# Loading a rotation table through ScalarE's queue, three slots sooner

## The chip, the cores and the metric

The kernel runs on one core of one Trainium2 chip. The metric is the device time of one execution in microseconds; lower is better. The core has five engines with a queue of instructions each: TensorE (PE, with the weight loads as PEld), VectorE (DVE), ScalarE (ACT), GpSimd (POOL) and SyncE (SP). They run side by side and wait for each other by semaphores. SyncE, ScalarE and GpSimd issue DMA transfers; 16 DMA engines carry these out. In the profile q1 is the DMA queue of SyncE's transfers, q10 that of ScalarE's, and q0 that of GpSimd's.

## The reference

The reference is an encoder trunk of two layers over 512 tokens of width 1024. Each layer normalizes the tokens, projects them once into mixer heads, memory query heads and a gate, attends, gates the heads, projects back and adds the result. The first layer's mixer is dilated window attention, the second's is grouped-query attention. The first layer's part that the change bears on is this:

```python
qkv = qkv.reshape(Bn, S, 3, N_A_GROUPS, A_HEADS, HEAD_DIM)
q = rmsnorm(qkv[:, :, 0], qn_g[:, None, :])
k = rmsnorm(qkv[:, :, 1], kn_g[:, None, :])
q = apply_rope(q, ang) * (HEAD_DIM ** -0.5)
k = apply_rope(k, ang)
```

Only the first 32 of the 128 columns of a head are rotated (`apply_rope` with 16 angles), so a token needs 16 cosines and 16 sines, and the norm gains qn_g and kn_g of the three groups for those 32 columns.

## The kernel before

**Tiling.** Tokens stand in four blocks of 128. A matrix product in float32 is made of three products in a shorter float: each weight tile wl (128x1024) is split by ScalarE into a high part wh (L333) and by VectorE into a low part wo (L347), and TensorE multiplies wh with the high and the low part of the activations (L178, L179) and wo with the high part (L182). The big projections (`s_chunk`) use the seven products of Strassen's scheme for 2x2 blocks, so sums of weight tiles are needed. Such sums are made by VectorE (L291) or by accumulating DMA transfers that GpSimd issues (L260, L296, L306). Plain weight loads are issued by SyncE (L260). Four wh and four wo tiles are kept in a ring.

**Order.** The order on every engine is written out by the program. A `Driver` counts slots; a slot ends when TensorE has done one group of products, which is 12 products of 512 columns in this part of the program. Side work is a generator that is given to the driver with a delay in slots and yields the number of slots until its next step. Within a slot the steps run in the order in which they were given. So slots fix the order of instructions on an engine, and not a time.

**The table.** `setup()` is such a generator, given with the delay `SET_AT`. Its first step issues three DMA loads: the table of cosines and sines (tabA, 128 rows of 1 KB, read as `(a i) f -> i a f` with i = 4, L1255) and the first 32 columns of the gains, broadcast to 128 partitions (grA, twice 128 x 3 rows of 128 B, L1256 for the queries' qn and L1257 for the keys' kn). Its second step scales the query gains on VectorE (L1263, which reads what L1256 loaded), and its third multiplies table and gains into the table that is used later (L1266, twice, which reads all three).

**Around it.** The first step falls in the projection of the first group's values. SyncE's queue holds weight loads and, at L1341, the stores of the finished value tiles to v0r in HBM. ScalarE's holds the casts L333, casts of activations (L671), and the copies L415 out of PSUM. VectorE's holds the low parts L347, sums of activations (L683, L685), low parts of activations (L674), the sums L438 out of PSUM, and parts of the memory keys and values (L753, L756, L790).

**Counters.** The transfers of SyncE and ScalarE use eight semaphores in turn, in the order in which the program names them; the instruction rows call them DMAHW0 to DMAHW7. A transfer waits until the one before it on its semaphore has landed. GpSimd's use eight others (DMASW). The suffix _49 means nothing here.

## Time and profile before

| What | Value |
|---|---|
| median of 3 runs | 933.24 us (933.13 to 934.04) |
| the profiled execution, its own time | 933.17 us |
| its span, first to last instruction | 931.4 us |
| TensorE busy | 924.8 us, 99% |
| VectorE busy | 801.7 us, 86% |
| ScalarE busy | 695.7 us, 75% |
| GpSimd busy | 360.5 us, 39% |
| packets of q1, q0, q10 | 60744, 20384, 1968 |
| granted TensorE clock | 1.0 |

Busy times are unions of an engine's instructions, without its sequencer's own work such as issuing a DMA. A timeline row has the start, the duration, the engine and line, the operation, the tiles as output <- inputs, and the number of instructions merged in it; in square brackets stands the idle time of the engine before it and what ended it. A `q` behind an engine's name marks its sequencer. A row of a DMA queue has its packets, their megabytes, and the time they took as a share of 16 engines; a packet is one row of a transfer, or one of the 4-byte marks with which a transfer reports its end.

### The profile page before, as it was taken

What the parts mean: (1) busy time and instruction counts of PE and PEld (TensorE: products, weight loads), DVE (VectorE), ACT (ScalarE), POOL (GpSimd) and SP (SyncE); (2) the same over time, 40 slices, a digit from 0 to 9 for tenths busy, and PEclk for the clock granted to TensorE, in tenths of its full rate; (3) what the DMA queues carried; (4) which work ended last, traced back from release to release, by engine and by line L of the source; (5) the groups of instructions that cost most, each with busy time, mean ns of one, the idle gap of its engine ahead of it and who ended that gap; (6) DMA issues with size and microseconds to landing.
All of it is one profiled execution on the core that took longest, in us unless ns stands there. A gap on an engine that the chain in (4) does not pass through costs nothing.

```text
span 931.4 us, 16276 instructions
## 1 busy us (share of the span) xinstructions
PE 924.8 (99%) x5471; PEld 814.7 (87%) x5471; DVE 801.7 (86%) x1457; ACT 695.7 (75%) x1725; POOL 360.5 (39%) x504
## 2 busy tenths in 40 slices
PE   9999999999999999999999999999999999999998
PEld 7789888888888888888889998888988999999886
DVE  6999677879888888979798989999898998789977
ACT  7775789677868686867776767757879887789774
POOL 4411425556564646464746102234252440110122
PEclk9999999999999999999999999999999999999999
DMA  9999948968686778686867899999985687785777
GB/s 351 389 264 331 300 127 218 319 146 247 162 248 166 249 160 271 159 272 135 241 178 207 231 261 271 289 320 331 289 219 114 178 233 178 201 227 116 200 162 181
DMA packets 83179, 212.85 MB, mean 229 GB/s; under 512 B 18960, under 2 KB 25752, under 8 KB 83096
## 3 DMA queue, kind: packets, MB, share of 16 engines
q1 hardware_dynamic: 60744, 141.16, 42.3%
q0 software_dynamic: 20384, 67.12, 39.1%
q10 hardware_dynamic: 1968, 3.54, 1.0%
q8 instruction: 43, 0.70, 0.3%
q14 instruction: 40, 0.33, 0.1%
HBM read 162.96 MB, written 12.65 MB: 189 GB/s over the span
## 4 chain that ended last, share of the span: by engine, by line
PE 91%; DVE 5%; DMA 2%; ACT 1%; SPq 0%; issue 0%; DVEq 0%; ACTq 0%
PE pj L178 24%; PE pj L179 24%; PE pj L182 24%; PE qT L716 3%; PE sa L1476 2%; PE oo L1585 2%; PE ptb L1819 1%; PE sa L1472 1%; DVE wo L347 1%; PE pt L1564 1%; DMA x<-in_x_dram 1%; DMA row<-in_norm_g_dram 1%; PE ob L178 1%; PE ob L182 1%; PE ob L179 1%; PE xT L589 1%
## 5 line engine op out<-in xcount | busy, mean ns | idle before, releaser
L347 DVE TENSOR_TENSOR wo<-wl,wh 128x1024 fp32r<-128x1024 f32 x253 | 308.8, 1225 | 5.6 <-ACT wh L333 5.6
L333 ACT CAST wh<-wl 128x1024 fp32r<-128x1024 f32 x253 | 267.3, 1061 | 27.5 <-PE pj L179 19.5
L178 PE MATMUL pj<-wh,hS 128*128 128x512 f32 (+1 forms) x416 | 154.5, 380 | 0.0
L179 PE MATMUL pj<-wh,hS 128*128 128x512 f32 (+1 forms) x416 | 148.9, 367 | 0.0
L178 PE MATMUL pj<-wh,h 128*128 128x512 f32 (+1 forms) x312 | 115.3, 378 | 0.0
L179 PE MATMUL pj<-wh,h 128*128 128x512 f32 (+1 forms) x312 | 111.6, 367 | 0.0
L536 POOL TENSOR_TENSOR rstd<-mse,half 128x4 f32<-128x4 f32 (+2 forms) x98 | 102.0, 1041 | 8.2
L182 PE MATMUL pj<-wo,hS 128*128 128x512 f32 (+1 forms) x416 | 99.5, 366 | 0.0
L179 PEld LDWEIGHTS pj<-wh,hS 128*128 128x128 f32 x416 | 78.7, 189 | 11.2
L178 PEld LDWEIGHTS pj<-wh,hS 128*128 128x128 f32 x416 | 78.6, 189 | 11.0
L535 POOL TENSOR_SCALAR mse<-hss 128x4 f32<-128x4 f32 (+1 forms) x88 | 45.6, 519 | 104.4 <-ACT junk L704 91.3
L182 PEld LDWEIGHTS pj<-wo,hS 128*128 128x128 f32 x416 | 72.4, 189 | 13.0 <-DVE wo L347 0.2
L704 ACT ACTIVATE junk<-sn 128x128 f32<-128x128 f32 x264 | 79.3, 310 | 3.4 <-DVE sn L428 3.4
L260 POOL DMA_DIRECT2D wl<-in_wall_dram x44 | 41.9, 982 | 95.4 <-DMA wl<-in_wall_dram 21.7
L1417 POOL TENSOR_TENSOR ta<-sn,tabs 128x128 f32<-128x128 f32 (+1 forms) x64 | 38.3, 605 | 104.0 <-DVE sn L709 80.4
L415 ACT COPY sn<-pj 128x512 f32<-128x512 f32 x122 | 67.2, 590 | 12.3 <-PE pj L182 12.3
L182 PE MATMUL pj<-wo,h 128*128 128x512 f32 (+1 forms) x312 | 74.5, 366 | 0.0
L306 POOL DMA_DIRECT2D wl<-wl x35 | 31.0, 895 | 109.2 <-DVE wo L347 48.7
L438 DVE TENSOR_TENSOR sn<-pj,sn 128x512 f32<-128x512 f32 x89 | 60.7, 683 | 6.5 <-PE pj L182 6.2
L179 PEld LDWEIGHTS pj<-wh,h 128*128 128x128 f32 x312 | 59.0, 189 | 8.4
L178 PEld LDWEIGHTS pj<-wh,h 128*128 128x128 f32 x312 | 59.0, 189 | 8.2
L296 POOL DMA_DIRECT2D wl<-wl x35 | 32.9, 964 | 78.7 <-DVE wl L291 18.9
(299 smaller groups left out, 2403.0 us busy)
## 6 DMA issues: line engine op xcount, KB each, us to landing
wl<-in_wall_dram SPq DMA_DIRECT2D x226, 512.0 KB, 7.4
wl<-wl POOLq DMA_DIRECT2D x70, 512.0 KB, 5.9
wl<-in_wall_dram POOLq DMA_DIRECT2D x48, 512.0 KB, 8.6
od<-o SPq DMA_DIRECT2D x9, 256.0 KB, 5.8
x<-in_x_dram SPq DMA_DIRECT2D x4, 512.0 KB
v0r<-sn SPq DMA_DIRECT2D x8, 256.0 KB, 8.5
v0d<-v0r SPq DMA_DIRECT2D x4, 512.0 KB
og<-od ACTq DMA_DIRECT2D x4, 512.0 KB
```

The costliest lines, as they stand in the source:

```text
L178: T.matmul(o, a, b, start=start, stop=False, skip_group_check=True)
L179: T.matmul(o, c, d, start=False, stop=False, skip_group_check=True)
L182: T.matmul(o, a, b, start=False, stop=stop, skip_group_check=True)
L260: queue.dma_start(t, wall[d], **how)
L333: A.copy(wh, self.tile[key])
L347: V.tensor_tensor(wo, self.tile[key], wh.bitcast(F32), ALU.subtract)
L415: A.copy(t_, b_)
L438: V.tensor_tensor(t_, b_, t_, ALU.subtract if q == "12" and late is None else ALU.add)
L535: G.tensor_scalar(e, ss, EPS, None, ALU.add)
L536: G.tensor_tensor(r, e, half[:, 0:n], ALU.pow)
L704: A.activation(jk, p[:, j * 128:(j + 1) * 128], AF.Square, scale=by, accum_out=ss[:, j:j + 1])
L1417: G.tensor_tensor(ta[:, 0:n], xn[:, 0:n, 0:32], ropeA[:, 0, b, s0:s0 + n], ALU.mult)
```

## The change

The three loads are issued by ScalarE, not SyncE, and `SET_AT` goes from 15 to 12 while the first yield goes from 4 to 7. The first step thus comes three slots sooner, and the second and third stay in their slots.

```diff
-BULK, ACTIVE, SET_AT, MEM_B, PREP_Y, PREP_B, HALF, SET_B = 2, 2, 15, 14, 1, 1, {"a": 3, "b": 3, "o": 0}, 12
+BULK, ACTIVE, SET_AT, MEM_B, PREP_Y, PREP_B, HALF, SET_B = 2, 2, 12, 14, 1, 1, {"a": 3, "b": 3, "o": 0}, 12
...
     def setup():
 
-        nc.sync.dma_start(tabA.rearrange("p b c d -> p (b c d)"), tab_a.rearrange("(a i) f -> i a f", i=4))
-        nc.sync.dma_start(grA[:, 0:3], qn_a[0:1, :, 0:32].to_broadcast([128, 3, 32]))
-        nc.sync.dma_start(grA[:, 3:6], kn_a[0:1, :, 0:32].to_broadcast([128, 3, 32]))
-        yield 4
+        nc.scalar.dma_start(tabA.rearrange("p b c d -> p (b c d)"), tab_a.rearrange("(a i) f -> i a f", i=4))
+        nc.scalar.dma_start(grA[:, 0:3], qn_a[0:1, :, 0:32].to_broadcast([128, 3, 32]))
+        nc.scalar.dma_start(grA[:, 3:6], kn_a[0:1, :, 0:32].to_broadcast([128, 3, 32]))
+        yield 7
```

On ScalarE the three loads enter behind the cast L333 that starts at 48.67 us in the profile before, in the projection of the first values (hS is an activation tile, f what it is cast from):

```order
 L671 CAST hS_623<-f_402 128x4x128
 L333 CAST wh<-wl 128x1024
+L1255 DMA tabA<-in_tab_a_dram 128x1x256
+L1256 DMA grA<-in_qn_a_dram 128x3x32
+L1257 DMA grA<-in_kn_a_dram 128x3x32
 L671 CAST hS_623<-f_456 128x4x128
 L333 CAST wh<-wl 128x1024
```

Nothing else moves on ScalarE; the cast L671 now stands behind three issues.

On SyncE, in the same part of the program, with what each transfer waits for, before the change:

```order
L1341 DMA v0r<-sn 128x512 [waits DMAHW5_49,DVE_49]
L1341 DMA v0r<-sn 128x512 [waits DMAHW6_49,DVE_49]
L260 DMA wl<-in_wall_dram 128x1024 [waits DMAHW7_49,PE_49]
L1255 DMA tabA<-in_tab_a_dram 128x1x256 [waits DMAHW0_49,Activation_49]
L1256 DMA grA<-in_qn_a_dram 128x3x32 [waits DMAHW1_49,PE_49]
L1257 DMA grA<-in_kn_a_dram 128x3x32 [waits DMAHW2_49]
L260 DMA wl<-in_wall_dram 128x1024 [waits DMAHW3_49]
L260 DMA wl<-in_wall_dram 128x1024 [waits DMAHW4_49]
L260 DMA wl<-in_wall_dram 128x1024 [waits DMAHW5_49]
L260 DMA wl<-in_wall_dram 128x1024 [waits DMAHW6_49,DMASW1_49,Activation_49]
L260 DMA wl<-in_wall_dram 128x1024 [waits DMASW5_49,DMAHW7_49,DVE_49,Activation_49]
```

And after it, where tabA, qn and kn have taken DMAHW5, 6 and 7 on ScalarE:

```order
L1341 DMA v0r<-sn 128x512 [waits DMAHW0_49,DVE_49]
L1341 DMA v0r<-sn 128x512 [waits DMAHW1_49,DVE_49]
L260 DMA wl<-in_wall_dram 128x1024 [waits DMAHW2_49,PE_49]
L260 DMA wl<-in_wall_dram 128x1024 [waits DMAHW3_49,PE_49]
L260 DMA wl<-in_wall_dram 128x1024 [waits DMAHW4_49,Activation_49]
L260 DMA wl<-in_wall_dram 128x1024 [waits DMAHW5_49,Activation_49]
L260 DMA wl<-in_wall_dram 128x1024 [waits DMAHW6_49,DMASW1_49,Activation_49]
L260 DMA wl<-in_wall_dram 128x1024 [waits DMASW5_49,DMAHW7_49,DVE_49,Activation_49]
```

The three loads are gone from SyncE's queue, and its fourth, fifth and sixth weight load behind the v0r stores now wait for the landing of tabA, qn and kn.

On VectorE, at slot 19, where the query gains are scaled:

```order
 L1261 TENSOR_SCALAR gc<-gc 128x2
 L1262 MEMSET gk 32x3 [waits DVE_49]
-L1263 TENSOR_SCALAR grA<-grA 128x96 [waits DMAHW1_49]
+L1263 TENSOR_SCALAR grA<-grA 128x96 [waits DMAHW6_49]
 L790 TENSOR_TENSOR vm<-vr,vm 128x512
```

VectorE's order is the same as before; L1263 waits for qn's new counter.

## The prediction

> **What bounds the kernel now.** I read the profile's page first (span, engines, DMA), then the timelines of SyncE, ScalarE, VectorE and TensorE around 50 us, where the change lies, and last the DMA queues in short windows. From the page:

> ```profile
> span 931.4 us, 16276 instructions
> PE 924.8 (99%) x5471; PEld 814.7 (87%) x5471; DVE 801.7 (86%) x1457; ACT 695.7 (75%) x1725; POOL 360.5 (39%) x504
> ...
> DMA  9999948968686778686867899999985687785777
> ```

> TensorE (PE) is the bound: 924.8 of 931.4 us. So a change away from TensorE can win only where TensorE stands still, and loses wherever it makes TensorE stand still. The DMA row shows the second fact that matters: in the first five slices (0 to 116 us) all DMA engines are nearly always busy. By stretches, with the columns PE, PEld, DVE, ACT, POOL, granted clock, DMA share, GB/s:

> ```profile
> 46.00:60.00 14.00, 14.00 (x67) 11.45 (x66) 13.44 (x17) 11.80 (x19) 2.61 (x3) 1.00 1.06 245
> 60.00:74.00 14.00, 14.00 (x64) 11.58 (x63) 13.97 (x22) 9.69 (x14) 2.17 (x3) 1.00 1.05 285
> 74.00:90.00 16.00, 16.00 (x130) 15.77 (x129) 13.87 (x17) 8.92 (x17) 3.58 (x5) 1.00 1.04 358
> ```

> From 46 to 90 us TensorE has no idle time to give back, VectorE is full too (13.97 of 14.00 us from 60 to 74), and the DMA share is above 1.

> **The removed issues.** SyncE's queue now:

> ```profile
> 16.06 21.95 SPq L260 DMA_DIRECT2D wl<-in_wall_dram  x18
> 52.43 0.92 SPq L1341 DMA_DIRECT2D v0r<-sn  x2
> ...
> 53.97 0.72 SPq L1255 DMA_DIRECT2D tabA<-in_tab_a_dram  x1
> 54.80 0.58 SPq L1256 DMA_DIRECT2D grA<-in_qn_a_dram  x1
> 55.43 4.72 SPq L1257 DMA_DIRECT2D grA<-in_kn_a_dram  x1
> 60.20 5.86 SPq L260 DMA_DIRECT2D wl<-in_wall_dram  x5
> ```

> Of these, three issues of 0.72, 0.58 and 4.72 us go, so the weight loads behind them may be issued up to 6.0 us sooner. On the time this is worth nothing: TensorE waits for no weight there (14.00 of 14.00 us), and the DMA engines have no free share. The same bytes move, in another order.

> **The added issues on ScalarE.** They stand behind the cast of 48.67 us and ahead of the cast L671:

> ```profile
> 48.67 1.05 ACT L333 CAST wh<-wl 128x1024 fp32r<-128x1024 f32 x1
> 51.11 0.62 ACT L671 CAST hS<-f 128x512 fp32r<-128x512 f32 x1 [1.39 <-DVE f L683]
> 52.92 0.68 DVE L674 TENSOR_TENSOR hS<-f,hS 128x512 fp32r<-128x512 f32 x1
> 53.52 1.22 DVE L347 TENSOR_TENSOR wo<-wl,wh 128x1024 fp32r<-128x1024 f32 x1
> 54.82 1.16 PE L182 MATMUL pj<-wo,hS 128*128 128x512 f32 x4
> ```

> The counters they wait for were last used by three of the 18 weight loads issued from 16 to 38 us, and not the last ones, so I expect no wait. At the first two SyncE durations, and 0.58 again for the third (same shape as the second), the three take 1.9 us, from 48.7 to 50.6 if the sequencer goes on once the cast is dispatched, to 51.6 if it waits for its end. The cast L671 waits for VectorE until 51.11 anyway, and its result is used at 52.92, so 1.2 us more are covered. Cost 0; the bounds are 0 and, with the 4.72 us row for the third issue, a cast that starts 3.6 us late (48.7 + 6.0 = 54.7). That would matter, because wo ends at 54.74 and TensorE takes it at 54.82: about 2.4 us. I take 0, since 4.72 us was met behind three bulk transfers, the table and the first gain rows in SyncE's queue, and ScalarE's queue is empty.

> **The transfers themselves.** Here I expect the loss. They change from SyncE's queue (q1) to ScalarE's (q10), at a moment when GpSimd's accumulating transfers (q0) fill the DMA engines. How queues share an engine is seen where a tiny transfer, a full-row transfer and all three queues meet accumulation:

> ```profile
> DMA packets 103, 0.22 MB, mean 217 GB/s; under 512 B 50, under 2 KB 50, under 8 KB 103
> ...
> q0 software_dynamic: 52, 0.21, 104.3%
> q1 hardware_dynamic: 51, 0.01, 9.4%
> ...
> q0 software_dynamic: 30, 0.10, 52.2%
> q1 hardware_dynamic: 31, 0.13, 36.0%
> q10 hardware_dynamic: 29, 0.06, 16.6%
> ```

> The first group is 456 to 457 us: 50 packets of under 512 B against 52 of accumulation. The second is 542 to 543 us: 30, 31 and 29. Every queue gets one packet per turn, however small it is. [...]

> So rows are what count, not bytes. Each gain load (grA) is 384 rows of 128 B, 24 on each of 16 engines, plus an end mark. The table is 128 rows of 1 KB read with the stride-4 index outermost. The profile's nearest transfer of that form, ds at L1511 (128 rows, outer index of four), leaves

> ```profile
> DMA packets 132, 0.00 MB, mean 4 GB/s; under 512 B 132, under 2 KB 132, under 8 KB 132
> ```

> in 347 to 348 us: 128 rows and four end marks, so four engines. I take the same for the table: 33 turns on four engines, then 25 for qn, 25 for kn. On those four, qn has landed after 58 turns.

> The turns, by the packets that q0 and q1 moved in 52.4:56, 56:62, 62:66 (q0 alone) and 66:73:

> ```profile
> q0 software_dynamic: 210, 0.76, 106.3%
> q1 hardware_dynamic: 5, 0.01, 0.9%
> ...
> q0 software_dynamic: 255, 0.92, 76.6%
> q1 hardware_dynamic: 290, 0.58, 28.4%
> ...
> q0 software_dynamic: 23, 0.06, 7.8%
> ...
> q0 software_dynamic: 228, 0.87, 62.0%
> q1 hardware_dynamic: 346, 1.17, 43.5%
> ...
> out_dram<-acc ACTq DMA_DIRECT2D x5, 256.0 KB, 2.5
> wl<-in_wall_dram SPq DMA_DIRECT2D x226, 512.0 KB, 7.4
> ds<-stp SPq DMA_DIRECT2D x16, 4.0 KB, 13.4
> ```

> Start: the v0r stores issued at 52.43 had moved next to nothing by 56 us (5 packets), so 3.6 us after 48.7, at 52.3. A packet of q1 in the last window, mostly 4 KB, takes 7 x 16 x 0.435 / 346 = 0.14 us; a 1 KB row of the table, a quarter of it, 0.04. To 56 us a turn of q0 is 3.6 x 16 / 210 = 0.27 us, with the row 0.31: 12 turns. To 62 us, with v0r in the round, 6 x 16 / 255 = 0.38, with the row 0.42: 14 turns. From 62 to 66 q0 is nearly empty now; it will be about 1 us longer (26 rows x 0.04): 2 turns, and then 3 us beside weight rows alone, 0.18 each: 16 turns. That makes 44 by 66 us: the table's 33, and 11 of qn's. From 66 us q0 is back: 7 x 16 / 228 = 0.49 us a turn, 0.50 with the small row, so the other 14 take 7.0 us, to 73.0. The count comes later than the last row; the issue-to-landing row of 2.5 us for out_dram bounds that tail. I take 2 of it, since the engines stay full here and each share above is a mean while the slowest of the four decides: qn is counted at 75.0. That a small transfer can need this long the row of ds shows: 4 KB, 13.4 us.

> **Who waits for it.**

> ```profile
> 68.93 0.20 DVE L1263 TENSOR_SCALAR grA<-grA 128x96 f32<-128x96 f32 x1
> ...
> 69.04 0.69 DVE L790 TENSOR_TENSOR vm<-vr,vm 128x512 fp32r<-128x512 f32 x1
> 69.65 0.69 DVE L438 TENSOR_TENSOR sn<-pj,sn 128x512 f32<-128x512 f32 x1
> 70.25 1.22 DVE L347 TENSOR_TENSOR wo<-wl,wh 128x1024 fp32r<-128x1024 f32 x1
> ...
> 83.09 0.95 DVE L1266 TENSOR_TENSOR tabs<-tabA,grA 128x768 f32<-128x768 f32 x1
> ...
> 74.42 1.07 PE L182 MATMUL pj<-wo,h 128*128 128x512 f32 x4
> ```

> The first reader, L1263, stays at slot 19 and comes up at 68.93, with no idle time before it today. It then waits 75.0 - 68.9 = 6.1 us, and VectorE's whole queue behind it: L790, the evacuation L438, and the low weight part of 70.25, ready at 71.47 and taken by TensorE at 74.42. That is 2.95 us of cover, so TensorE stands 6.1 - 2.95 = 3.1 us at its L182, and no later work gives this back, since it is the bound. The two later low parts have about 4 and 5.7 us of cover (they follow back to back) and slip no further than the first.

> SyncE's later loads: the fourth, fifth and sixth after the v0r stores wait for the counters of tabA, qn and kn, where they waited for old stores and loads before. The two that wait for qn and kn are then issued after 75 us, not at 63 and 66. VectorE adds those tiles with L291 at 77 and 80 us, by now 83 and 86; the first has 8 us for the 7.4 us that the row of wl gives as the median, so I cost this at 0 and keep 2 us above. L1266, which reads kn, moves to 89: kn's 25 further turns at 0.2 to 0.5 us end by then.

> **Sum.** 0 (SyncE) + 0 (ScalarE's issues) + 3.1 (VectorE's wait past its cover) = 3.1 us. The profiled execution took 933.17 us, 1.8 beyond its span; the median is 933.24, so nothing is to be scaled: 936.3. Own range: a start 2 us earlier (5 to 6 turns, 2.8 us) gives 0.3 us, a start 1.5 us later and the 2 us of SyncE's loads give 5.9: 933.5 to 939.2.

> **Rivals.**
> - *Hidden* (not slower): qn is there before 68.9. It decides at 68.93 + 2.95 = 71.9: landed by then, TensorE sees nothing. For it: a table on all 16 engines would need 8 + 1 + 25 = 34 turns, done at about 64 by the count above; or many rows to a turn. Against it: four end marks, and 50 against 52. Price 0 to +0.2 us: 933.3. [...]
> - *ScalarE blocked*: the third issue takes 4.72 us again, or twice that. Once: L671 3.6 us late, 1.2 covered, TensorE 2.4 us late at 54.82; VectorE then reaches L1263 at 71.3, waits 3.7 us, 0.8 past its cover: 3.2 in all, as above by another road. Twice: 7.1 us at 54.82, and VectorE reaches L1263 after qn: 940.3. For it: the row of 55.43. Against: an empty queue.
> - *Faster*: SyncE's six us bring weights sooner and ScalarE's small waits go. TensorE has 0.00 idle us from 46 to 90; the 54.82 row, which starts 0.08 us after its wo, is all there is: 933.1.

> **Chances.** VectorE's wait 0.57; hidden 0.30; ScalarE blocked 0.10; faster 0.03. This kernel's measurement tells apart about 0.2%, 1.9 us. Of the first case a fifth falls below that, of the third nothing: slower 0.57 x 0.8 + 0.10 = 0.56. Of the rest, faster by over 0.2% has 0.02, the last rival being bounded far below it: same 0.42. I forecast 936.3; the range reaches from the hidden case to the likeliest one's upper end, 933.0 to 939.2.

> **What would show it.** Three ACTq issues from about 48.7 us, each under 1 us, and L671 still at 51.1; q10 in the DMA windows from 52 to beyond 70 us, its rows about as many as q0's; SyncE with a gap before its fourth weight load until tabA lands near 65; VectorE idle before L1263 for about 6 us, released by the grA load; PE idle some 3 us before L182 at 74.4, and none elsewhere. Wrong if L1263 has no idle time before it (hidden), or if the idle time of TensorE stands at 54.8 us (ScalarE).

## The result, and the profile after

The changed kernel takes 937.39 us (median of 6 runs, 936.70 to 939.54), the kernel before 933.64 us in the same sessions (933.01 to 934.95): the ratio is 1.0042, 95% interval 1.0029 to 1.0055, or 3.75 us lost. The profiled execution was the longest of the six, 939.54 us; a second profiled execution of the same kernel, shown further below, took 937.51 us. One of the eleven executions of the kernel with the gains first, below, took 3286.82 us; it stands in no ratio. From the page of the first profiled execution:

```profile
span 937.8 us, 16276 instructions
PE 927.3 (99%) x5471; PEld 816.5 (87%) x5471; DVE 802.0 (86%) x1457; ACT 696.0 (74%) x1725; POOL 363.1 (39%) x504
```

TensorE has the same 5471 products, but is busy for 2.5 us longer, and the span is 6.4 us longer. ScalarE and SyncE around the moved loads:

```profile
48.30 0.66 ACTq L1255 DMA_DIRECT2D tabA<-in_tab_a_dram  x1
49.06 0.52 ACTq L1256 DMA_DIRECT2D grA<-in_qn_a_dram  x1
49.62 0.58 ACTq L1257 DMA_DIRECT2D grA<-in_kn_a_dram  x1
50.80 0.62 ACT L671 CAST hS<-f 128x512 fp32r<-128x512 f32 x1 [1.47 <-DVE f L683]
...
53.14 23.56 SPq L260 DMA_DIRECT2D wl<-in_wall_dram  x6
```

The three issues take 1.8 us in all, and the cast behind them, at 50.80 us, is no later than before (51.11). SyncE, which issued such loads at 53 and from 60 to 66 us, now stands in the middle of them: six loads take it 23.56 us. VectorE, and TensorE with its waits:

```profile
68.86 0.06 DVE L1262 MEMSET gk<- 32x3 f32 x1
75.59 0.21 DVE L1263 TENSOR_SCALAR grA<-grA 128x96 f32<-128x96 f32 x1 [6.67 <-DMA grA<-in_qn_a_dram]
76.92 1.22 DVE L347 TENSOR_TENSOR wo<-wl,wh 128x1024 fp32r<-128x1024 f32 x1
...
78.19 2.08 PE L182 MATMUL pj<-wo,h 128*128 128x512 f32 x4 [3.93 <-DVE wo L347]
80.07 0.41 PE L178 MATMUL pj<-wh,h 128*128 128x256 f32 x1
```

VectorE stands 6.67 us for the row qn, and TensorE 3.93 us for the low weight part behind it. The next rows were not foreseen: the four products of L182 take 2.08 us where they took 1.07 before, and the products of 256 columns 0.41 where they take 0.28. The same stretch in steps of 3.41 us, with busy TensorE, granted clock, DMA share and GB/s, first for this execution, then for the second one:

```profile
70.12:73.54 3.42, 3.42 (x17) 1.00 0.85 242
73.54:76.95 3.41, 0.72 (x4) 1.00 0.18 63
76.95:80.36 3.41, 2.17 (x6) 0.50 0.89 296
80.36:83.78 3.42, 3.42 (x18) 0.50 1.02 373
83.78:87.19 3.41, 3.41 (x30) 1.00 1.06 267
```

```profile
73.54:76.96 3.42, 0.76 (x4) 1.00 0.42 145
76.96:80.37 3.41, 3.24 (x11) 0.50 0.85 292
80.37:83.78 3.41, 3.41 (x30) 1.00 1.02 318
```

In the kernel before, where the clock is 1.00 from 5.7 to 930.7 us, the products of 256 columns begin with this row:

```profile
75.33 0.28 PE L178 MATMUL pj<-wh,h 128*128 128x256 f32 x1
```

In both executions the step that TensorE mostly stood through (0.72 and 0.76 us busy) is followed by one at half the clock; in the first, where that one has 2.17 us of work, by a second half-clock step, in the second, where it has 3.24, by none. In the second execution:

```profile
74.53 0.21 DVE L1263 TENSOR_SCALAR grA<-grA 128x96 f32<-128x96 f32 x1 [5.34 <-DMA grA<-in_qn_a_dram]
...
77.13 2.08 PE L182 MATMUL pj<-wo,h 128*128 128x512 f32 x4 [2.83 <-DVE wo L347]
```

Against the profile before, TensorE's groups of products (each begins with L178) start 0.3 us early from 36 to 74 us in both executions. From 81 us to the end they are 6.4 us late in the first and 4.3 in the second. So stand and clock make 6.7 us in the first (3.93, and 2.8 of clock) and 4.6 in the second (2.83, and 1.7 of clock). The clock's part is what is left when the stand is taken off; TensorE's busy time, 2.5 and 1.6 us above that of the kernel before, bears it out. Of the six timed runs five had a mean granted clock of 0.996 or 0.997, as these two have; the quickest, 936.70 us, had 0.999.

### The profile page after: what moved, and what is told of

Its sections match the earlier page's. It is cut to its first block, busy times and chain, and to the rows that moved or that the text cites. A ratio compares the mean times of both kernels' runs of the same rounds, so it can differ in the third digit from the quotient of the medians.

```text
span 937.8 us, 16276 instructions
## 1 busy us (share of the span) xinstructions
PE 927.3 (99%) x5471; PEld 816.5 (87%) x5471; DVE 802.0 (86%) x1457; ACT 696.0 (74%) x1725; POOL 363.1 (39%) x504
## 4 chain that ended last, share of the span: by engine, by line
PE 86%; DVE 7%; DMA 4%; ACT 2%; issue 1%; POOL 0%; SPq 0%; ACTq 0%; DVEq 0%
PE pj L182 23%; PE pj L178 23%; PE pj L179 22%; DMA grA<-in_kn_a_dram 3%; PE qT L716 2%; DVE wo L347 2%; PE sa L1476 2%; PE oo L1585 2%; PE ptb L1819 1%; PE sa L1472 1%; PE pt L1564 1%; DMA x<-in_x_dram 1%; PE ob L178 1%; PE ob L182 1%; PE ob L179 1%; DMA wl<-in_wall_dram 1%
## 5 line engine op out<-in xcount | busy, mean ns | idle before, releaser
L347 DVE TENSOR_TENSOR wo<-wl,wh 128x1024 fp32r<-128x1024 f32 x253 | 309.3, 1227 | 5.7 <-ACT wh L333 5.6
L333 ACT CAST wh<-wl 128x1024 fp32r<-128x1024 f32 x253 | 267.1, 1061 | 34.4 <-PE pj L179 16.1
L178 PE MATMUL pj<-wh,hS 128*128 128x512 f32 (+1 forms) x416 | 154.5, 380 | 0.0
L178 PE MATMUL pj<-wh,h 128*128 128x512 f32 (+1 forms) x312 | 116.7, 382 | 0.0
L179 PE MATMUL pj<-wh,h 128*128 128x512 f32 (+1 forms) x312 | 112.9, 370 | 0.0
L536 POOL TENSOR_TENSOR rstd<-mse,half 128x4 f32<-128x4 f32 (+2 forms) x98 | 102.7, 1048 | 8.2
L182 PE MATMUL pj<-wo,hS 128*128 128x512 f32 (+1 forms) x416 | 99.5, 366 | 0.0
L178 PEld LDWEIGHTS pj<-wh,hS 128*128 128x128 f32 x416 | 78.6, 189 | 11.0
L182 PEld LDWEIGHTS pj<-wo,hS 128*128 128x128 f32 x416 | 72.4, 189 | 13.0 <-DVE wo L347 0.3
L182 PE MATMUL pj<-wo,h 128*128 128x512 f32 (+1 forms) x312 | 75.6, 369 | 3.9 <-DVE wo L347 3.9
L260 POOL DMA_DIRECT2D wl<-in_wall_dram x44 | 41.9, 982 | 92.9 <-DMA wl<-in_wall_dram 32.2
L306 POOL DMA_DIRECT2D wl<-wl x35 | 31.0, 895 | 115.9 <-DVE wo L347 55.6
L179 PEld LDWEIGHTS pj<-wh,h 128*128 128x128 f32 x312 | 60.1, 193 | 8.4
L178 PEld LDWEIGHTS pj<-wh,h 128*128 128x128 f32 x312 | 60.1, 193 | 8.3
L182 PEld LDWEIGHTS pj<-wo,h 128*128 128x128 f32 x312 | 55.0, 191 | 14.1 <-DVE wo L347 4.3
L438 DVE TENSOR_TENSOR sn<-pj,sn 128x512 f32<-128x512 f32 x89 | 60.9, 685 | 6.3 <-PE pj L182 6.0
## 6 DMA issues: line engine op xcount, KB each, us to landing
wl<-in_wall_dram SPq DMA_DIRECT2D x226, 512.0 KB
wl<-wl POOLq DMA_DIRECT2D x70, 512.0 KB, 5.8
wl<-in_wall_dram POOLq DMA_DIRECT2D x48, 512.0 KB, 8.5
od<-o SPq DMA_DIRECT2D x9, 256.0 KB
x<-in_x_dram SPq DMA_DIRECT2D x4, 512.0 KB
v0r<-sn SPq DMA_DIRECT2D x8, 256.0 KB
v0d<-v0r SPq DMA_DIRECT2D x4, 512.0 KB
og<-od ACTq DMA_DIRECT2D x4, 512.0 KB
```

The source lines that it names most:

```text
L178: T.matmul(o, a, b, start=start, stop=False, skip_group_check=True)
L179: T.matmul(o, c, d, start=False, stop=False, skip_group_check=True)
L182: T.matmul(o, a, b, start=False, stop=stop, skip_group_check=True)
L260: queue.dma_start(t, wall[d], **how)
L333: A.copy(wh, self.tile[key])
L347: V.tensor_tensor(wo, self.tile[key], wh.bitcast(F32), ALU.subtract)
```

## The experiments

The first theory was the prediction's: the row qn, in a queue behind the table, is late, and VectorE's wait for it is the whole loss. Four kernels took it apart, each timed in turn with the kernel before. In the first, only VectorE's reader moves.

```diff
-        V.memset(gk[0:32, :], 1.0)
+        V.memset(gk[0:32, :], 1.0); yield 1
         V.tensor_scalar(grA[:, 0:3], grA[:, 0:3], QS, None, ALU.mult)
-        yield 6
+        yield 5
```

> Only VectorE's gain step (L1263) moves, one slot on, behind four other instructions of VectorE; the three transfers stay on ScalarE's queue at slot 12. Theory (the whole loss is VectorE waiting at L1263 for the row qn): the step is met at about 72 us, waits 3.5 us for the same landing at 75.6, and the next product with wo, ready at about 77.0, is wanted by TensorE at 77.2: no stand, granted clock 1.00 throughout, 933.3 to 934.0 us. Rival (the small rows on a second queue, or SyncE standing 23 us at its weight loads, hold up the weights): the wait at L1263 is not what counts, and 937.4 us stays.

Measured: 938.41 us against 933.83, ratio 1.0051 (1.0037 to 1.0065). The loss stays. The reader, and TensorE's waits (us in total, times, longest):

```profile
75.16 0.21 DVE L1263 TENSOR_SCALAR grA<-grA 128x96 f32<-128x96 f32 x1 [3.06 <-DMA grA<-in_qn_a_dram]
```

```profile
PE qT L1381 <- DVE sn L709: 1.9, 1, 1.9
PE pj L178 <- DVE sn L438: 1.2, 1, 1.2
```

The stand at L182 is gone, as the theory said; in its place TensorE waits 1.2 us for an evacuation of VectorE, which is 3 us behind, and 1.9 us near 103 us for L709. So the theory falls in its word "whole": something else is late as well. A second profiled execution was to show whether the clock is in it:

> The kernel with L1263 one slot later once more, for a second profiled execution. In the first one TensorE stood 1.2 us for an evacuation near 86 us and 1.9 us for rstd near 103, and the time was 936.9, while the median of its runs is 938.4. If the landing of qn alone varies: the same two stands, 1 to 4 us in sum, clock 1.00, 935.5 to 938.5 us. If a stand falls across a whole window of the clock: one or two windows of 3.4 us at 0.5, and 938.5 us or more.

Measured: 936.54 us, waits of 0.38 us for L438 and 2.32 us for L709, no half-clock step. That is the first case. Both profiled executions are among the quicker ones: of the six timed runs, three at mean granted clocks of 0.996 to 0.998 took 938.5 to 940.8 us. Where the clock fell in those was not seen.

The next kernel puts the gain rows ahead of the table in the same queue.

```diff
+        nc.scalar.dma_start(grA[:, 0:3], qn_a...)
+        nc.scalar.dma_start(grA[:, 3:6], kn_a...)
         nc.scalar.dma_start(tabA..., tab_a.rearrange("(a i) f -> i a f", i=4))
-        nc.scalar.dma_start(grA[:, 0:3], qn_a...)
-        nc.scalar.dma_start(grA[:, 3:6], kn_a...)
```

> Same queue, same slot; only the order of the three transfers changes: the two gain rows ahead of the table. Theory (qn is late because it stands behind the table's 33 turns on four engines): qn needs 25 turns on all engines, 26 are had by 62 us, so it lands at 62 to 63, well before 68.9; kn lands at about 69, the table at 75 to 77 with use at 89: no wait, 933.3 to 934.0 us. Rival (a small-row transfer on ScalarE's queue is late whatever its place): qn lands after 69 and at least 936 us remain.

Measured: 935.71 us against 933.83, ratio 1.0019 (1.0010 to 1.0028): half of the loss goes. VectorE does not wait at L1263 (68.78 us), as expected, but TensorE stands once more near 103 us. The chain of work that ended last says why; its columns are start, duration, what:

```profile
49.62 27.79 DMA tabA<-in_tab_a_dram
...
77.50 0.33 SPq L260
...
85.02 13.96 DMA wl<-in_wall_dram
...
99.61 0.65 POOL wl L260
...
102.11 1.05 POOL rstd L536
...
103.18 0.70 DVE sn L709
```

Now it is the table that lands late, at 77.4 us. SyncE's third held weight load shares its counter and goes out at 77.50, not at 65.7 as before; all loads and stores behind it on SyncE shift, up to the load of 85.02, which was issued at 83.09 before. GpSimd must see that last weight landed before it can issue the accumulating load L260, and behind L260 stands rstd (L536), which VectorE's L709 and then TensorE's L1381 need. In the kernel before, and here:

```profile
96.35 0.93 POOL L260 DMA_DIRECT2D wl<-in_wall_dram  x1 [7.95 <-DMA wl<-in_wall_dram]
101.39 0.60 PE L1381 MATMUL qT<-ident,sn 128*128 128x128 f32 x4
```

```profile
99.61 0.93 POOL L260 DMA_DIRECT2D wl<-in_wall_dram  x1 [9.63 <-DMA wl<-in_wall_dram]
103.93 0.66 PE L1381 MATMUL qT<-ident,sn 128*128 128x128 f32 x4 [2.59 <-DVE sn L709]
```

So the theory became: one cause, the late landing of the moved loads, with two ways to TensorE, by VectorE's L1263 and by SyncE's held loads. In the changed kernel TensorE is already 4.3 to 6.4 us late when the second way would stop it, so that only the first shows. They are not added; the longer one counts. Two things stay open: no kernel took the shared counter away by itself, and of the 3.3 us that GpSimd's L260 is late here, the later issue gives 1.9; why the load then lands later still was not followed.

The third kernel leaves the order alone and spreads the table.

```diff
-        nc.scalar.dma_start(tabA..., tab_a.rearrange("(a i) f -> i a f", i=4))
+        [nc.scalar.dma_start(tabA[i * 32:(i + 1) * 32]..., tab_a.rearrange("(a i) f -> i a f", i=4)[i]) for i in range(4)]
```

> Same queue, slot and order, but the table comes as four transfers of 32 partitions each instead of one with an outer index of 4. Theory (the table's rows lie on four DMA engines alone): now every engine has 3 turns for each quarter, 12 in all instead of 33 on four of them, then 25 for qn: 37 turns, of which 26 are had by 62 us and the rest at 2 turns per us or better by 66 to 67. Landing at 65 to 67.5, before 68.9: no wait, 933.3 to 934.2 us; the three more issues on ScalarE (1.8 us) end at about 52, where the cast L671 still has its result ready at 52.9. Rival (the rows are spread over the engines anyway, the queue is just slow): qn still lands near 75 and 937 us stays.

Measured: 934.46 us, ratio 1.0006 (0.9997 to 1.0015). VectorE comes to L1263 at 71.10 and does not wait. All but some 0.6 us is back with the same queue, slots and bytes. What is left shows on ScalarE, where six issues now stand ahead of the cast L671:

```profile
49.40 2.69 ACTq L1255 DMA_DIRECT2D tabA<-in_tab_a_dram  x4
52.18 0.64 ACTq L1256 DMA_DIRECT2D grA<-in_qn_a_dram  x1
52.86 1.24 ACTq L1257 DMA_DIRECT2D grA<-in_kn_a_dram  x1
54.14 0.62 ACT L671 CAST hS<-f 128x512 fp32r<-128x512 f32 x1 [3.71 <-DMA tabA<-in_tab_a_dram]
```

The cast starts 3.0 us later than before (51.11), and in this execution TensorE lost 1.4 us there: the rival "ScalarE blocked", which the three issues of the change do not bring about, and six do.

The fourth keeps the slots of the change and gives the loads back to SyncE.

```diff
-        nc.scalar.dma_start(...)
+        nc.sync.dma_start(...)
```

> The three transfers go back to SyncE's queue, but stay at slot 12. They then stand behind the 18 weight loads (issued by 38 us) and ahead of the stores of v0r, and may be issued at about 38 to 50 us instead of 54. Theory (the queue, not the slot, makes the loss): in the queue they follow the weights one after another and land 4 to 10 us sooner than before; no wait at L1263, 933.2 to 934.0 us, and SyncE does not stand for them later. Rival (the three slots make the loss by putting the transfers into a busier stretch): 936 us or more.

Measured: 934.94 us, ratio 1.0011 (1.0003 to 1.0020): neither 933.2 to 934.0 nor 936. VectorE does not wait for qn. TensorE waits twice, 0.39 and 0.67 us, for evacuations of VectorE (L438). They come late by way of a store: the two stores to v0r now stand in SyncE's queue behind the three loads, and ScalarE's next copy out of PSUM has to wait until one of them has landed.

```profile
64.54 0.59 ACT L415 COPY sn<-pj 128x512 f32<-128x512 f32 x1 [3.76 <-DMA v0r<-sn]
```

In the kernel before this copy follows the one of 60.47 us without a wait. Behind the late copy ScalarE's cast L671 is late, and VectorE idles 3.65 us for it, until 66.63 us. So three slots sooner cost 1.1 us in SyncE's queue, and the other queue the rest. That was turned round next, with the new queue and the old slots:

```diff
-... SET_AT ... = 2, 2, 12, ...
+... SET_AT ... = 2, 2, 15, ...
-        yield 7
+        yield 4
```

> Only the queue of the change is kept: the three loads on ScalarE's queue at slot 15, with the use at slot 19 as before. Theory: ScalarE issues them at about 58.5 us, behind the cast L671, and the rows start 2.5 to 4 us later; of the 58 turns that qn needs, some 16 are had by 66 us, the rest at 0.36 to 0.5 us until TensorE stands, and quicker from then: qn lands at 80 to 84 us, VectorE waits 11 to 15 us at L1263, TensorE 8 to 12, and the clock term of the change's profiled run (2.6 us) may come on top: 942 to 948 us. So the queue makes the loss, and the three slots sooner soften it. Rival (the slot makes the loss, by the stretch into which it puts the transfers): 933 to 935 us.

Measured: 940.48 us against 933.50, ratio 1.0071 (1.0057 to 1.0085): the direction of the theory, below its band.

```profile
53.25 0.66 ACTq L1255 DMA_DIRECT2D tabA<-in_tab_a_dram  x1
...
77.10 0.21 DVE L1263 TENSOR_SCALAR grA<-grA 128x96 f32<-128x96 f32 x1 [7.89 <-DMA grA<-in_qn_a_dram]
...
79.70 1.65 PE L182 MATMUL pj<-wo,h 128*128 128x512 f32 x3 [5.01 <-DVE wo L347]
```

I had read the time of issue from the place behind a cast; the issue came at 53.25, not 58.5, and qn at 77.1. It came 5 us later than in the change and landed 1.5 to 2.6 us later. The three slots sooner thus save about 3 us of what the new queue costs here.

Rows against bytes was the next question: the gains fetched whole, in a third of the rows and four times the bytes.

```diff
+    grF = tabs[:, 1280:2048].rearrange("p (s c) -> p s c", s=6)
-        nc.scalar.dma_start(grA[:, 0:3], qn_a[0:1, :, 0:32].to_broadcast([128, 3, 32]))
+        nc.scalar.dma_start(grF[:, 0:3]..., qn_a[0:1].rearrange("o s c -> o (s c)").to_broadcast([128, 384]))
...
-        V.tensor_scalar(grA[:, 0:3], grA[:, 0:3], QS, None, ALU.mult)
-        yield 6
+        V.tensor_scalar(grA[:, 0:3], grF[:, 0:3, 0:32], QS, None, ALU.mult)
+        yield 6; V.tensor_copy(grA[:, 3:6], grF[:, 3:6, 0:32])
```

> Queue, slot, order and the table as in the change; the gain rows are fetched whole, 384 numbers in one piece for each partition, instead of three pieces of 32: four times the bytes, a third of the rows (8 and an end mark on each engine instead of 24 and one). They land in the second half of ropeA, which is free until L1266, and one copy of 128x96 (about 0.2 us on VectorE) is added. Theory (rows count, not bytes): the table's 33 turns end at 65.5 to 66.5 as now, qn's 9 follow at 0.36 us each, at 69 to 70, kn's at 72 to 73. L1263 waits 0 to 1.5 us, inside its cover of 3; SyncE's loads go on at 72 to 73 instead of 76, so the later wait for rstd near 100 us goes too: 933.5 to 934.8 us. Rival (bytes count): the gain rows take longer than now, qn after 76, and 938 us or more.

Measured: 934.35 us against 933.50, ratio 1.0008 (1.0000 to 1.0017). ScalarE's queue from 52 to 76 us, in the change, with the table in quarters, and with whole gain rows (packets, MB, share):

```profile
q10 hardware_dynamic: 932, 0.23, 4.8%
```

```profile
q10 hardware_dynamic: 992, 0.23, 5.0%
```

```profile
q10 hardware_dynamic: 420, 0.52, 6.5%
```

932 is 128 rows of the table and 4 marks, and twice 384 rows and 16 marks; 992 has 64 marks for the table's four parts, 16 for each. With one mark for each engine, as I read them, the table in one transfer lies on four engines; its single rows, further below, agree. With 420 packets, though of 0.52 MB, qn is there at 69.6:

```profile
69.60 0.25 DVE L1263 TENSOR_SCALAR grA<-tabs 128x96 f32<-128x96 f32 x1 [1.02 <-DMA tabs<-in_qn_a_dram]
...
102.44 0.65 PE L1381 MATMUL qT<-ident,sn 128*128 128x128 f32 x4 [1.46 <-DVE sn L709]
```

Rows it is, not bytes. The kn row, 51 turns deep, still lands near 74 us (72 to 73 expected), so 1.46 us of the second way are left. Then both cures together, the edits of the table in quarters and of the whole rows:

> Both cures at once: the table as four transfers of 32 partitions (12 turns on every engine) and the gain rows fetched whole (9 turns each): 30 turns for all three, against 83 on four engines in the change. Theory (the loss is the late landing alone, by way of two waits, VectorE's at L1263 and SyncE's held weight loads): everything lands by 62 to 66 us, VectorE does not wait at L1263, SyncE's third held load goes out by 66 as before, and GpSimd's weight issue near 96 us is not late, so rstd does not hold up TensorE near 101 us: 933.3 to 934.3 us, of which up to 0.7 us for the three more issues on ScalarE, which the table by quarters alone showed. Rival (a second queue costs something in itself, whatever its rows): 934.5 us or more, as in both cures taken singly.

Measured: 933.37 us against 933.81, ratio 0.9997 (0.9989 to 1.0006).

```profile
69.86 0.25 DVE L1263 TENSOR_SCALAR grA<-tabs 128x96 f32<-128x96 f32 x1
...
96.95 0.93 POOL L260 DMA_DIRECT2D wl<-in_wall_dram  x1 [7.38 <-DMA wl<-in_wall_dram]
101.97 0.60 PE L1381 MATMUL qT<-ident,sn 128*128 128x128 f32 x4
```

Neither way is left, and neither is the loss. This is the change as it was given, on the same queue in the same slots, with fewer and better spread rows. It ties with the kernel before and does not beat it: TensorE had no idle time here to be won. (The third held load went out at 67.0, not by 66; nothing waited for it.)

Last, the clock. The reader is put one slot sooner, to lengthen the stand:

```diff
-        yield 7
+        yield 6
...
-        yield 6
+        yield 7
```

> The change with VectorE's first reader L1263 one slot sooner (slot 18); transfers unmoved. It is then met at about 65 us, with the products with wo of 66.7 and later behind it, until qn lands at 75 to 75.6: TensorE, which wants that product at 71.7, stands 6.5 to 8 us. If the loss at this place is just the wait, the time is 933.6 + 6.5 to 8, 940 to 942 us. If a stand also sets the granted clock to 0.5 for a fixed time of about 6.8 us, which cost 2.6 us in the change's profiled run, it is 942.5 to 944.5 us; if that lower clock lasts longer after a longer stand, more than 945 us.

Measured: 941.20 us (937.38 to 942.55), ratio 1.0076 (1.0057 to 1.0095); the profiled execution took 942.55.

```profile
67.97:71.38 3.41, 1.96 (x9) 1.00 1.05 260
71.38:74.80 3.42, 0.00 (x0) 1.00 0.58 163
74.80:78.21 3.41, 1.35 (x3) 0.50 0.78 207
78.21:81.62 3.41, 3.41 (x9) 0.50 0.76 258
```

```profile
PE pj L178 <- DVE sn L438: 6.9, 1, 6.9
```

The stand is 6.9 us and still costs two half-clock steps: in this execution the fixed case. The median lies in the band without a clock term, though three of the four runs had a mean granted clock of 0.996, as the profiled one; the fourth, 937.38 us, had 1.000. So the stand was presumably shorter in some runs, and one run did without the half clock; neither was seen in a trace. The step with 1.96 us of work was followed by one at 1.00.

And the changed kernel again, from which the second profile above comes:

> The changed kernel once more, for a second profiled execution. If the stand at L182 and the clock of 0.5 behind it are there in every execution: a stand of 3 to 4 us near 74 us, and 0.5 for about 6.8 us. If the clock term comes in some executions alone: the stand near 3 us, the clock at 1.00, and the time near 937.

Measured: 937.51 us, a stand of 2.83 us, and 0.5 for one step of 3.41 us, not two: between the two cases. The clock term is there in both profiled executions; its size differs.

## Why the prediction was right, point by point

- **Removed issues, worth 0.** Confirmed: no wait of TensorE goes away from 46 to 90 us.
- **Added issues on ScalarE, cost 0.** Confirmed: 0.66, 0.52 and 0.58 us, and L671 at 50.80.
- **The transfers: one packet for each turn, the table on four engines, qn counted at 75.0.** Confirmed: qn is used at 75.59 and 74.53. The equal counts that the prediction leans on, 50 against 52, would come out of many rows to a turn too, if every queue took as many. The single packets in the trace of the changed kernel tell the two apart: of the table's four engines three start a row together, at 53.16 to 53.21, at 53.52 to 53.58 and at 53.89 to 53.94 us. These are 0.36 us apart, about the time of one accumulating packet (0.33 us) and one row of the table (0.06 us). The fourth starts its rows at 52.75, 53.27 and 53.79 us, 0.52 apart, about the time of these two kinds (there 0.33 and 0.05 us) and one 4 KB packet of SyncE's queue (0.17 us). So each queue gave one row to a turn there. The three kernels with fewer turns ahead of qn (gains first, table in quarters, whole rows) all brought it by 71 us. The table has 4 marks with its outermost 4, and 64 as four parts of 32 rows.
- **The count of turns.** That 75.0 came out within 0.6 us is luck in part, since two sizes were off in opposite ways. The count has 11 of qn's turns done by 66 us. SyncE's fourth load, which waits for the table, went out at 66.53; and at 66 us 190 and 173 gain rows were still to come in the two executions, of the 192 that qn and kn have on four engines, so none to about five of qn's turns were done. The turns left then took less than the 0.50 us each that the count gives them. Nor did "the engines stay full here" hold: the DMA share fell to 0.18 and 0.42 in the step from 73.54 us.
- **VectorE's wait of 6.1 us and TensorE's stand of 3.1.** Confirmed in kind: 6.67 and 3.93 us, 5.34 and 2.83.
- **SyncE's held loads, cost 0 and 2 above.** This step was mis-sized, and its place was wrong. I followed the loads only to the sums that VectorE makes at 77 and 80 us and not to GpSimd, whose queue holds rstd behind a weight load 20 us later. By itself it stops TensorE for 2.59 us (gains first; 1.8 us by the ratio). It did not spoil the sum because TensorE is already late when it would act; that too is luck.
- **"No later work gives this back."** True, but more is lost: the granted clock behind the stand was no term of the sum. It was worth 2.8 and 1.7 us in the two profiled executions. So the 936.3 lack 1.1 us to 937.39 (0.7 beside the 3.75 lost). In the second execution, whose time is near the median, the 3.1 us of stand were 2.83, the clock added 1.7, and a start 0.3 us quicker took a little off. The forecast was near because the stand was about right and the missing term small.
- **The range.** Its upper end does not follow from its terms. If a start 2 us earlier is worth 2.8 us, one 1.5 us later is worth 2.1, and with the 2 us of SyncE's loads that makes 3.1 + 2.1 + 2 = 7.2 us over the kernel before and not 5.9. The measured loss lies inside either.
- **The rivals.** *Hidden* fails at its own mark: qn came at 74.5 to 75.6, not by 71.9. *Faster* has nothing for it. *ScalarE blocked* did not come with three issues.

## What to carry to other kernels

Before moving a small load to another queue, count its rows and the engines that they lie on, not its bytes: beside the busy queues here each row took a turn of its own (0.36 to 0.52 us for rows of the table from 52.8 to 53.9 us), and with the outermost index of 4 all 128 lay on four engines (4 marks; 64 in quarters). Then list every instruction that will wait for its landing, by data and by a shared counter alike, and follow each through whole queues to the bound engine; taking away the first wait may only uncover the second. If such loads must move, fetch whole rows in a shape that uses all engines (16 marks a transfer), which here paid the loss back (933.37 us against 933.81).

## What the runs showed of the hardware that was not expected

```profile
99.11:102.53 3.42, 2.23 (x10) 1.00 1.02 418
102.53:105.94 3.41, 2.01 (x11) 1.00 1.08 261
```

In the kernel with the reader later, stands of 1.2 and 1.9 us left the clock at 1.00 as well. That it counts where a stand falls, beside its length, is my reading of these stands; no run moved a stand of one length to another place.

**A late counter reached far.** With the gains first, a weight load that went out at 77.5 us instead of 65.7, since the table held its counter, stopped TensorE at 101 to 104 us, by way of GpSimd and VectorE, in work that doesn't read the table. This rests on the rows of the chain above.
